# Two hybrid decoder layers: the rounded and the rest half of each weight chunk made by two DMAs and one ScalarE copy

## The chip, the cores and the metric

The kernel runs on one core of a Trainium2 chip. TensorE multiplies matrices, VectorE and ScalarE work on tiles element by element, GpSimd does small work of the same sort, and SyncE and GpSimd issue transfers (DMAs) between HBM and SBUF, the core's working memory. Each engine runs its own list of instructions in order and waits on semaphores for the others. The metric is the device time of one execution in microseconds; a time is the median of several runs.

## The reference

Two layers over 512 tokens of width 1024, all in float32. Cut to what matters here:

```python
for l in range(2):
    h = rms_norm(x, attn_norm_g[l])
    a_q, a_k, a_v, b_q, b_k, b_v, c_u, gates = split(h @ w_in[l])    # 1024 -> 9728 columns
    oa = diff_attention(rope(norm(a_q)), rope(norm(a_k)), a_v)       # 4 heads
    ob = dilated_window_attention(b_q, b_k, b_v)                     # 3 windows x 4 heads
    oc = s5_branch(c_u)                                              # state space scan, gated
    g = sigmoid(gates + b_gate[l])
    merged = g[0] * (oa @ w_br_a[l]) + g[1] * (ob @ w_br_b[l]) + g[2] * (oc @ w_br_c[l])
    x = x + merged @ w_out[l]
    a, b = split(rms_norm(x, ffn_norm_g[l]) @ w_up[l])               # 1024 -> 2 x 2816
    x = x + (silu(conv3(a)) * b) @ w_down[l]
```

The weights are 172 MB of float32, read once. The result has to keep float32 accuracy.

## The kernel before

TensorE multiplies in float32r, a float32 that is rounded to fewer bits. To keep the accuracy each operand is split into hi (the value rounded to float32r) and lo (what is left), and a product is the sum of three: hi\*hi, hi\*lo and lo\*hi (`mm3`, L172, products on L177 to L179). The activations are split when they are made (`hth` and `htl` for the normalised input, `gh` and `brh`/`brl` for others). The weights are split when they are loaded.

The weights come in 328 chunks of [128, 1024] float32 (512 KB), 164 in a layer, in the order in which the program wants them; the host packs them so. `chunk` (L151) makes the two halves: SyncE issues the load into a slot of the pool `raw` (3 slots, L155), ScalarE copies it to `whi` with rounding (5 slots, L158), and VectorE writes the difference raw - hi to `wlo` (5 slots, L159). A slot is free again when the last product that reads it has ended.

Chunks are used in two ways. In "t" and "t2" products (SSM input, gates and their branches, up projection) a chunk is used for 24 products in a row and is then done. In "n" products (`slab`, L162: q, k, v, output and down projection) three or four chunks make a slab of up to 1024 rows by 512 columns, and the slab is used for four tiles of 128 tokens, one after the other: each tile's pass goes through all chunks of the slab (6 products each), so a chunk is done only in the fourth pass. A boundary below is the place where one slab ends and the next begins.

Attention and the state space branch are side work: generators whose steps are put between the units of the projections (`tick`). The program is then given to a scheduling layer that sets each engine's order and all semaphores; GpSimd, ScalarE and VectorE each have one fixed list. GpSimd computes, among other things, the powers for the norms (`nr`, L410, of a tile of the input; `qr`, L477, of q and k heads) and clears buffers. At the start the input rows x are loaded by SyncE, ScalarE sums their squares (`junk`, L406), GpSimd makes the factor `nr`, VectorE the normalised rows `hn` (L413), TensorE transposes them (`ptp`, L184), and ScalarE and VectorE split them into `hth` and `htl`.

Of the kernel before, what the change touches and what calls it, by code (L numbers as in the profile page):

```python
"""Two hybrid decoder layers (differential attention, dilated window attention, S5 SSM, gated
merge, convolutional gated MLP) on one core.

float32 matrix products run as three float32r products: an operand is split exactly into
hi (rounded to float32r) and lo (the rest), and hi*hi + hi*lo + lo*hi accumulate in PSUM.
"""
# [10 lines left out]
F32 = mybir.dt.float32  # L17
# [3 lines left out]
AF = mybir.ActivationFunctionType  # L21
ALU = mybir.AluOpType
AX = mybir.AxisListType.X
MUL, ADD, SUB, MAX, MIN = ALU.mult, ALU.add, ALU.subtract, ALU.max, ALU.min
# [11 lines left out]
# S5 channels within a tile of 8 groups x 16 channels: partition = channel * 8 + group  # L36
UPERM = np.arange(512).reshape(4, 8, 16).transpose(0, 2, 1).reshape(512)

# columns of the small per-layer parameters
PK_BG, PK_GT, PK_SUB, PK_CW, PK_CB, PK_D, PK_BGLU, PK_N = 0, 24, 28, 29, 95, 117, 121, 125  # L40

BUFS = dict(raw=3, whi=5, wlo=5, qkv=20, acc=9, tmp=10, brh=1, brl=1, ct=1, gn=1)

# steps of side work per unit of a projection: SSM, attention
# [3 lines left out]
class Stream:  # L48
    """side work in steps: a step advances every running generator by one stage and starts the
    next one, so that the stages of successive generators are interleaved"""  # L50
# [26 lines left out]
class Alone:  # L77
    """a generator that starts when all before it have ended, and lets no other run beside it"""
# [5 lines left out]
class Net:  # L84
# [66 lines left out]
    def chunk(self, *spec):  # L151
        i = len(self.specs)
        self.specs.append(spec)
        raw = self.slot("raw", "raw", (128, 1024))
        self.nc.sync.dma_start(raw, self.io["wpk"][i])  # L155
        hi = self.slot("whi", "whi", (128, 1024), F32R)
        lo = self.slot("wlo", "wlo", (128, 1024), F32R)
        self.A.copy(hi, raw)  # L158
        self.V.tensor_tensor(lo, raw, hi.bitcast(F32), op=SUB)  # L159
        return hi, lo  # L160

    def slab(self, w, l, k0, nk, c0, before=None):  # L162
        """chunks for [nk*128, 512] of a weight; -> list over k of (hi, lo) [128, 512]"""
# [9 lines left out]
    def mm3(self, out, pairs):  # L173
        """out = sum over (stationary hi, lo), (moving hi, lo)"""
# [34 lines left out]
    def sincos(self, sin, cos, x, cols):  # L209
        """sin and cos of x [128, cols] (may overwrite x)"""  # L210
# [37 lines left out]
    def setup(self):  # L248
# [11 lines left out]
        # halves for sigmoids by tanh  # L260
# [3 lines left out]
        # columns for evacuating transposed q, k: gains times the score scale  # L264
# [5 lines left out]
        # angles: rope A (4 tiles x 8), rope B (2 orders x 4 tiles x 16), S5 (L x 16)  # L270
# [14 lines left out]
        # S5 scalars of both layers  # L285
# [18 lines left out]
        # f = (lambda - 1) / a  # L304
# [15 lines left out]
        # mag^8, and the unit phase exp(8 i theta)  # L320
# [12 lines left out]
    def layer_lambda(self, l):  # L333
        """lambda of the differential attention"""
# [17 lines left out]
    def layer_tables(self, l):  # L352
        """rope tables with gains and score scale; powers of the S5 lambda"""
# [17 lines left out]
        # powers of lambda, d = 0..8  # L371
# [8 lines left out]
    def cmul_step(self, tab, n, first, g):  # L380
        """tab[.., first+n : first+2n] = tab[.., first : first+n] * (element first+n-1 from `first`=1,
        or the n-th power kept apart): used for tables of powers that start at power 1"""
# [828 lines left out]
```

## Time and profile before

| | us |
|---|---|
| median of 3 runs (2149.47 to 2150.98) | 2149.77 |
| span of the profiled execution, first to last instruction | 2149.5 |
| TensorE busy | 2118.8 |
| VectorE busy | 1163.7 |
| ScalarE busy | 869.8 |
| GpSimd busy | 149.3 |

The profile gives the execution by its span; the median of the runs is 0.3 us above that. Busy times of engines overlap and don't add up to the span. A product's row lasts about 0.39 us while the next starts some 0.23 us later, since products are pipelined; distances between starts are what counts. The DMA share is the mean busy share of the core's 16 DMA engines. The TensorE clock was granted in full throughout (1.00).

### The profile page before, as it was taken

The page shows a single profiled execution, that of the slowest core. Times are in us where ns is not written, and L with a number is a line of the kernel's source. Part 1 is how long each engine was busy: PE and PEld are TensorE (multiplying, and loading weights), DVE is VectorE, ACT ScalarE, POOL GpSimd, SP SyncE. Part 2 cuts the span into 40 slices and gives each one's busy share as a digit, 9 for nine tenths or more (in the row PEclk, how much of TensorE's full clock was granted, in tenths as well). Part 3 has the DMA queues.
Part 4 walks back from the last instruction along what each step waited for, and adds up shares of the span by engine and source line. Part 5 has one row for each costly group of instructions (what it writes and reads, how often), then busy time and mean ns, then how long its engine had stood idle before and what let it go on. Part 6 is the DMA issues. An engine that isn't in the chain of part 4 may idle for free.

```text
span 2149.5 us, 28401 instructions
## 1 busy us (share of the span) xinstructions
PE 2118.8 (99%) x10742; PEld 1787.5 (83%) x10742; DVE 1163.7 (54%) x2589; ACT 869.8 (40%) x1789; POOL 149.3 (7%) x299
## 2 busy tenths in 40 slices
PE   7999999999999999999999999999999999999999
PEld 5877899988888888888888778999888888888887
DVE  6757565556544653544447575554564446445353
ACT  4355555463232432323334546464532324223131
POOL 1211111100000000000002102010000000000000
PEclk9999999999999999999999999999999999999999
DMA  5331221533433323323342312224334323233231
GB/s 185 99 100 40 60 81 59 136 113 99 137 98 93 108 92 95 98 89 98 118 123 64 96 42 68 85 68 123 113 108 129 102 73 108 88 106 92 77 118 59
DMA packets 97257, 206.40 MB, mean 96 GB/s; under 512 B 40544, under 2 KB 45408, under 8 KB 97120
## 3 DMA queue, kind: packets, MB, share of 16 engines
q1 hardware_dynamic: 97120, 204.58, 30.8%
q8 instruction: 85, 1.39, 0.3%
q14 instruction: 52, 0.43, 0.1%
HBM read 193.01 MB, written 11.53 MB: 95 GB/s over the span
## 4 chain that ended last, share of the span: by engine, by line
PE 88%; DVE 5%; ACT 4%; POOL 1%; DMA 1%; issue 1%; SPq 0%; ACTq 0%; DVEq 0%; POOLq 0%
PE pacc L179 26%; PE pacc L177 26%; PE pacc L178 26%; PE ptp L184 2%; PE ps L542 1%; PE po L639 1%; PE ps L615 1%; ACT qn L483 1%; PE ps L863 1%; DMA raw<-wpk 1%; ACT sq L474 1%; DVE wlo L159 1%; POOL qr L477 1%; PE ps L860 1%; PE ps L698 1%
## 5 line engine op out<-in xcount | busy, mean ns | idle before, releaser
L158 ACT CAST whi<-raw 128x1024 fp32r<-128x1024 f32 x328 | 343.7, 1054 | 676.6 <-PE pacc L178 403.9
L159 DVE TENSOR_TENSOR wlo<-raw,whi 128x1024 fp32r<-128x1024 f32 x328 | 399.0, 1223 | 401.0 <-ACT whi L158 394.4
L179 PE MATMUL pacc<-hth,wlo 128*128 128x512 f32 (+1 forms) x1200 | 460.7, 384 | 0.0
L177 PE MATMUL pacc<-hth,whi 128*128 128x512 f32 (+1 forms) x1200 | 458.6, 383 | 0.5 <-ACT hth L421 0.5
L178 PE MATMUL pacc<-htl,whi 128*128 128x512 f32 (+1 forms) x1200 | 458.7, 382 | 0.2
L177 PE MATMUL pacc<-whi,hth 128*128 128x512 f32 x768 | 319.8, 418 | 0.0
L178 PE MATMUL pacc<-wlo,hth 128*128 128x512 f32 x768 | 308.4, 402 | 3.2 <-DVE wlo L159 3.2
L179 PE MATMUL pacc<-whi,htl 128*128 128x512 f32 x768 | 310.4, 404 | 0.0
L178 PEld LDWEIGHTS pacc<-htl,whi 128*128 128x128 f32 x1200 | 225.4, 188 | 46.6 <-DVE htl L422 0.6
L177 PEld LDWEIGHTS pacc<-hth,whi 128*128 128x128 f32 x1200 | 225.1, 188 | 45.0 <-ACT hth L421 1.0
L179 PEld LDWEIGHTS pacc<-hth,wlo 128*128 128x128 f32 x1200 | 225.5, 188 | 43.8
L178 PEld LDWEIGHTS pacc<-wlo,hth 128*128 128x128 f32 x768 | 192.3, 251 | 18.9 <-DVE wlo L159 4.1
L179 PEld LDWEIGHTS pacc<-whi,htl 128*128 128x128 f32 x768 | 191.4, 249 | 16.5
L177 PEld LDWEIGHTS pacc<-whi,hth 128*128 128x128 f32 x768 | 191.3, 249 | 15.6 <-ACT hth L421 0.2
L177 PE MATMUL pacc<-whi,gh 128*128 128x512 f32 x352 | 139.9, 397 | 0.0
L178 PE MATMUL pacc<-wlo,gh 128*128 128x512 f32 x352 | 139.3, 396 | 0.0
L973 DVE TENSOR_TENSOR x<-x,pacc 128x512 f32<-128x512 f32 x64 | 44.0, 687 | 158.9 <-PE pacc L179 158.9
L178 PEld LDWEIGHTS pacc<-wlo,gh 128*128 128x128 f32 x352 | 66.1, 188 | 16.5
L177 PEld LDWEIGHTS pacc<-whi,gh 128*128 128x128 f32 x352 | 66.2, 188 | 16.0
L179 PE MATMUL pacc<-whi,brh 128*128 128x512 f32 x192 | 76.3, 397 | 0.0
L477 POOL TENSOR_TENSOR qr<-qr,mhalf 128x4 f32<-128x4 f32 (+1 forms) x64 | 75.6, 1181 | 5.3
L474 ACT ACTIVATE sq<-pacc 128x128 f32<-128x128 f32 x192 | 50.6, 284 | 41.1 <-PE pacc L179 40.9
(302 smaller groups left out, 2871.0 us busy)
## 6 DMA issues: line engine op xcount, KB each, us to landing
raw<-wpk SPq DMA_DIRECT2D x328, 512.0 KB, 3.7
x<-x SPq DMA_DIRECT2D x16, 256.0 KB, 6.0
gn<-ng SPq DMA_DIRECT2D x4, 512.0 KB, 5.8
u_d<-uS SPq DMA_DIRECT2D x8, 256.0 KB, 2.8
u<-u_d SPq DMA_DIRECT2D x8, 256.0 KB, 4.9
y_d<-ys SPq DMA_DIRECT2D x8, 256.0 KB, 2.2
ym<-y_d SPq DMA_DIRECT2D x8, 256.0 KB, 4.6
um<-u_d SPq DMA_DIRECT2D x8, 256.0 KB, 4.0
```

Source lines behind the costliest of these rows:

```text
L158: self.A.copy(hi, raw)
L159: self.V.tensor_tensor(lo, raw, hi.bitcast(F32), op=SUB)
L177: self.PE.matmul(out, lhsT=ah, rhs=bh, start=i == 0, stop=False)
L178: self.PE.matmul(out, lhsT=ah, rhs=bl, start=False, stop=False)
L179: self.PE.matmul(out, lhsT=al, rhs=bh, start=False, stop=i == n - 1)
L184: self.PE.transpose(tp[:, b * 128 : b * 128 + 128], src[:, b * 128 : b * 128 + 128], self.ident)
L474: A.activation(sq[:, h * dh : h * dh + dh], av[:, h], AF.Square, accum_out=ss[:, h : h + 1])
L477: G.tensor_tensor(r, r, self.mhalf[:, :heads], op=ALU.pow)
L483: A.activation(qv[:, h], qv[:, h], AF.Copy, scale=r[:, h : h + 1])
L542: PE.matmul(reg, lhsT=q[64 * j : 64 * j + 64, h * 128 : h * 128 + 128], rhs=k[kt][64 * j : 64 * j + 64, h * 128 : h * 128 + 128], start=kt ...
L615: PE.matmul(s[:, c : c + 128], lhsT=q[:, h * 128 : h * 128 + 128], rhs=k[kb][:, h * 128 : h * 128 + 128], start=h == h0 and b == 0, stop=F ...
L973: self.V.tensor_tensor(xt[t][s], xt[t][s], acc, op=ADD)
```

## The change

A chunk no longer has a raw slot. GpSimd issues a DMA that reads the float32 chunk and writes it to `whi` as float32r, so that the DMA does the rounding. ScalarE writes -hi into `wlo`. A second DMA, issued by GpSimd too, reads the same float32 chunk from HBM again and adds it onto that slot: `wlo` = raw - hi. VectorE's subtraction is gone. The three raw slots become two more for `whi` (7) and one more for `wlo` (6).

```diff
-BUFS = dict(raw=3, whi=5, wlo=5, qkv=20, acc=9, tmp=10, brh=1, brl=1, ct=1, gn=1)
+BUFS = dict(whi=7, wlo=6, qkv=20, acc=9, tmp=10, brh=1, brl=1, ct=1, gn=1)
...
     def chunk(self, *spec):
         i = len(self.specs)
         self.specs.append(spec)
-        raw = self.slot("raw", "raw", (128, 1024))
-        self.nc.sync.dma_start(raw, self.io["wpk"][i])
         hi = self.slot("whi", "whi", (128, 1024), F32R)
         lo = self.slot("wlo", "wlo", (128, 1024), F32R)
-        self.A.copy(hi, raw)
-        self.V.tensor_tensor(lo, raw, hi.bitcast(F32), op=SUB)
+        self.G.dma_start(hi, self.io["wpk"][i])
+        self.A.activation(lo, hi.bitcast(F32), AF.Copy, scale=-1.0)
+        self.G.dma_start(lo, self.io["wpk"][i], accum_op=ADD)
         return hi, lo
```

The rest of the diff takes out comments. Lines after the first few move by one: the load of hi is L156 of the changed kernel, the negated copy L157, the adding DMA L158.

What stands in the queues, at the two places that matter below. First the start. VectorE's list before begins with the subtraction of the first chunk, ahead of the cast of the identity and of the normalised rows hn:

```order
L159 TENSOR_TENSOR wlo_111<-raw_108,whi_110 128x1024
L243 CAST identr_69<-ident_64 128x128
L413 SCALAR_TENSOR_TENSOR hn_90<-x_73,nr_86,gn_77 128x512
L413 SCALAR_TENSOR_TENSOR hn_91<-x_75,nr_86,gn_77 128x512
L251 CAST identb_279<-identr_69 128x128
```

GpSimd's list in the changed kernel at the same place; `nr_86` is the factor of the first row tile (three instructions, L407 to L409), `whi_108`, `_144`, `_149`, `_154` and `wlo_109`, `_145` are the halves of the first four chunks:

```order
L156 DMA whi_108<-wpk 128x1024
masks.py:199 ISA
masks.py:199 AFFINE_SELECT ident_64<-ident_64 128x128
L407 TENSOR_TENSOR nr_86<-nss_81 128x1
L158 DMA wlo_109<-wpk 128x1024
L408 TENSOR_SCALAR nr_86<-nr_86 128x1
L156 DMA whi_144<-wpk 128x1024
L409 TENSOR_TENSOR nr_86<-nr_86,mhalf_71 128x1
L156 DMA whi_149<-wpk 128x1024
L156 DMA whi_154<-wpk 128x1024
L407 TENSOR_TENSOR nr_122<-nss_117 128x1
L158 DMA wlo_145<-wpk 128x1024
```

VectorE's hn no longer follows a subtraction, but the factor that it needs now ends behind the first adding DMA, which waits for the negated copy of the first chunk, and so do the loads of the chunks behind it.

Second, the boundary in the down projection of layer one. GpSimd's list in the changed kernel; `whi_8309`, `_8314`, `_8319` and `_8324` are the four chunks of the new slab, `wlo` with a number one higher their lo halves, `whi_8435` and `whi_8469` the next chunks:

```order
L156 DMA whi_8314<-wpk 128x1024
L158 DMA wlo_8310<-wpk 128x1024
L156 DMA whi_8319<-wpk 128x1024
L158 DMA wlo_8315<-wpk 128x1024
L156 DMA whi_8324<-wpk 128x1024
L158 DMA wlo_8320<-wpk 128x1024
L156 DMA whi_8435<-wpk 128x1024
L158 DMA wlo_8325<-wpk 128x1024
L156 DMA whi_8469<-wpk 128x1024
```

Before, SyncE's list held the loads into the raw slots at this place, one per chunk, and VectorE's the subtractions between the additions of the residual (`raw_8451` to `raw_8469` are the new slab's chunks):

```order
L973 TENSOR_TENSOR x_5952<-x_5952,pacc_8399 128x512
L159 TENSOR_TENSOR wlo_8460<-raw_8457,whi_8459 128x1024
L159 TENSOR_TENSOR wlo_8466<-raw_8463,whi_8465 128x1024
L159 TENSOR_TENSOR wlo_8472<-raw_8469,whi_8471 128x1024
L973 TENSOR_TENSOR x_5956<-x_5956,pacc_8425 128x512
```

The load of the fourth chunk (`whi_8324`) waits for the release of the first chunk of the old slab, seven chunks earlier; its adding DMA (`wlo_8325`) stands one load further on.

## Rows read from the trace of the kernel before

**Rows 1.** Page, part 1: busy time of each engine, share of the span, instructions.
```profile
PE 2118.8 (99%) x10742; PEld 1787.5 (83%) x10742; DVE 1163.7 (54%) x2589; ACT 869.8 (40%) x1789; POOL 149.3 (7%) x299
```

**Rows 2.** Page, part 5: line, operation | busy us, mean ns | idle before.
```profile
L158 ACT CAST whi<-raw 128x1024 fp32r<-128x1024 f32 x328 | 343.7, 1054 | 676.6 <-PE pacc L178 403.9
L159 DVE TENSOR_TENSOR wlo<-raw,whi 128x1024 fp32r<-128x1024 f32 x328 | 399.0, 1223 | 401.0 <-ACT whi L158 394.4
...
L477 POOL TENSOR_TENSOR qr<-qr,mhalf 128x4 f32<-128x4 f32 (+1 forms) x64 | 75.6, 1181 | 5.3
```

**Rows 3.** Waits of TensorE: who waited for whom, us in total, times, longest.
```profile
PE ptp L184 <- DVE hn L413: 13.2, 3, 12.5
PE pacc L178 <- DVE wlo L159: 3.2, 2, 1.6
```

**Rows 4.** DMA queue and weight loads: share; form, ns min/median/max; us to landing.
```profile
q1 hardware_dynamic: 97120, 204.58, 30.8%
...
L155 SPq DMA_DIRECT2D raw<-wpk x328: 327/328/3961, 2.1 to 2103.1; - x164
...
DMA to landing us min/median/max: 3.2/3.7/8.2
```

**Rows 5.** Timeline of ScalarE, up projection: start, us, engine, operation [idle before].
```profile
896.73 1.05 ACT L158 CAST whi<-raw 128x1024 fp32r<-128x1024 f32 x1 [3.90 <-PE pacc L178]
...
907.72 1.05 ACT L158 CAST whi<-raw 128x1024 fp32r<-128x1024 f32 x1 [3.90 <-PE pacc L178]
```

**Rows 6.** Timeline of TensorE, down projection: old slab’s first chunk, new slab’s fourth.
```profile
953.18 0.39 PE L179 MATMUL pacc<-whi,brh 128*128 128x512 f32 x1
...
962.05 0.39 PE L178 MATMUL pacc<-wlo,gh 128*128 128x512 f32 x1
```

**Rows 7.** Timeline of ScalarE at the same place.
```profile
953.62 1.05 ACT L158 CAST whi<-raw 128x1024 fp32r<-128x1024 f32 x1 [16.85 <-PE pacc L179]
955.02 1.05 ACT L158 CAST whi<-raw 128x1024 fp32r<-128x1024 f32 x1 [0.35 <-PE pacc L179]
956.42 1.06 ACT L158 CAST whi<-raw 128x1024 fp32r<-128x1024 f32 x1 [0.35 <-PE pacc L179]
959.79 1.06 ACT L158 CAST whi<-raw 128x1024 fp32r<-128x1024 f32 x1 [2.31 <-DMA raw<-wpk]
```

**Rows 8.** Timeline of TensorE: the same two products at the first and last boundary.
```profile
84.03 0.39 PE L179 MATMUL pacc<-whi,htl 128*128 128x512 f32 x1
...
93.32 0.40 PE L178 MATMUL pacc<-wlo,hth 128*128 128x512 f32 x1
...
2018.99 0.39 PE L179 MATMUL pacc<-whi,brh 128*128 128x512 f32 x1
...
2027.86 0.40 PE L178 MATMUL pacc<-wlo,gh 128*128 128x512 f32 x1
```

**Rows 9.** Timeline of the start.
```profile
6.00 0.56 POOL L410 TENSOR_TENSOR nr<-nr,mhalf 128x1 f32<-128x1 f32 x1
...
9.31 1.05 ACT L158 CAST whi<-raw 128x1024 fp32r<-128x1024 f32 x1 [4.42 <-DMA raw<-wpk]
...
10.39 1.23 DVE L159 TENSOR_TENSOR wlo<-raw,whi 128x1024 fp32r<-128x1024 f32 x1 [10.39 <-ACT whi L158]
...
11.67 1.41 DVE L413 SCALAR_TENSOR_TENSOR hn<-x,nr,gn 128x512 f32<-128x512 f32 x2
...
12.46 1.97 PE L184 MATMUL ptp<-identr,hn 128*128 128x128 f32 x8 [12.46 <-DVE hn L413]
...
17.70 0.39 PE L178 MATMUL pacc<-wlo,hth 128*128 128x512 f32 x1
```

**Rows 10.** Busy us (count) of PE, PEld, DVE, ACT, POOL; PEclk; DMA share; GB/s.
```profile
50.00:450.00 400.00, 394.24 (x2290) 348.48 (x2289) 250.84 (x765) 209.54 (x567) 62.61 (x111) 1.00 0.29 86
...
720.00:1075.00 355.00, 354.66 (x1582) 290.14 (x1581) 170.28 (x201) 112.48 (x143) 1.88 (x6) 1.00 0.32 100
...
1120.00:1515.00 395.00, 389.31 (x2267) 344.18 (x2266) 236.20 (x669) 207.16 (x565) 61.19 (x106) 1.00 0.28 83
```

## The prediction, made before the changed kernel ran

> **What bounds the kernel now.** I read the busy times first. TensorE is busy for 2118.8 of 2149.5 us, VectorE for 1163.7, ScalarE for 869.8, GpSimd for 149.3 [rows 1]. TensorE is the bound nearly everywhere, so work taken from VectorE saves time only where TensorE waits for it. Second, the table of waits: what TensorE itself waits for VectorE's lo half comes to 3.2 us in 2 waits, and 13.2 us go to the first transposes, which wait for the normalised rows hn [rows 3]. Third, the busy times by stretch: between 50 and 450 us TensorE is idle for 400 - 394.24 = 5.8 us, between 1120 and 1515 us, the same attention stage in layer two, for 5.7 us, and in the gated MLP between 720 and 1075 us for 0.3 us [rows 10]. All that can be won outside the start is therefore about 11.5 us, 0.5%.
>
> What can be lost is large: every product needs a chunk of weights, and a chunk lasts 2149.5 / 328 = 6.55 us on average. So the fourth reading was how long a weight slot takes from its release to its next need. In the up projection chunks are released every 5.5 us (three casts, each at a release, between 896.73 and 907.72) [rows 5], and with 6 slots a lo half has about five such steps, 27 us, to be made. The tight places are elsewhere. Where a slab of four chunks follows a slab of four with nothing between, all four slots of the old slab stay in use until its last token tile, and then come free 1.4 us apart.
>
> The clearest one is in the down projection. The last product that reads the first chunk of the old slab starts at 953.18; the first product that reads the lo half of the fourth chunk of the new slab starts at 962.05 [rows 6]. That is 8.87 us, for seven chunks further on: exactly the depth of the new hi pool. I matched all 8016 products with their chunks by the program's order and took this distance for every chunk. Twelve chunks (six in each layer, the same six) have 8.8 to 10.5 us: 9.3, 9.3, 10.5, 8.8, 9.0 and 8.9. The first of the twelve is 84.03 to 93.32, the last 2018.99 to 2027.86 [rows 8]. Two more have 11.8, six have 14 to 15, all others more than 17. TensorE's order in the changed kernel keeps these twelve boundaries.
>
> Before the change the same boundary was met because the raw chunk was already there: the cast starts at 953.62, 0.44 us after the last product's start, and the next ones at 955.02 and 956.42, one per release [rows 7]; cast and subtraction take 1.05 + 1.22 us [rows 2].
>
> **The change part by part.**
>
> VectorE loses 328 subtractions of 1223 ns, 399.0 us [rows 2]. On TensorE's path this is worth the 3.2 us of direct waits [rows 3]; I take -4, for some of the small waits in attention that follow from a shorter VectorE queue. The bounds are 0 and -11.5.
>
> ScalarE's cast of 1054 ns [rows 2] becomes a negated copy of the same 128x1024 elements, from SBUF to SBUF as before: same price, 0.
>
> SyncE loses 328 issues. GpSimd gains 656. An issue takes SyncE 0.33 us [rows 4]; GpSimd's nearest row is a 1.18 us instruction [rows 2]. I take 1.0 us: 656 us, and with its 149.3 us GpSimd stays below 40% busy. Nothing is lost by that alone. What matters is that its queue is in order: an accumulating DMA waits there for ScalarE's negated copy, and the next load and the small powers of the q and k norms stand behind it. By the order shown above the boundary loads stand in a workable sequence, so I add nothing for that except at the start.
>
> The chain of a chunk becomes serial: load, negated copy, second DMA. At the boundary: release (0.44 after the last product's start), load of hi, 0.05, copy 1.05, 0.05, second DMA. A plain chunk lands 3.7 us after its issue (3.2 to 8.2) [rows 4]; the trace has no load that rounds, none that adds, and none issued by GpSimd. For hi I take 3.7 + 1.0 for the issue = 4.7. The lower end is 3.7, the upper the slowest plain landing, 8.2. For lo the DMA must also read the slot that it adds to. A chunk occupies the 16 DMA engines for 30.8% x 2149.5 / 204.58 MB x 0.524 MB = 1.7 us [rows 4], so I take 4.7 + 1.7 = 6.4; lower end 3.7, upper 8.2 + 1.7 = 9.9.
>
> The chain is 0.44 + 4.7 + 0.05 + 1.05 + 0.05 + 6.4 = 12.7 us. Against the budgets TensorE is late by 3.4, 3.4, 2.2, 3.9, 3.7 and 3.8 in each layer, and 0.9 at the boundary of 11.8: 21.3, and twice that is **+43 us**. As a check by load: at 953.6 the engines get hi, lo, hi, lo, that is 1.7 + 3.4 + 1.7 + 3.4 = 10.2 us of work before the needed lo is there, which with the 2.0 us that a plain landing has beyond its 1.7 ends near 966, as the chain says (953.18 + 12.7 = 965.9). At the lower end the chain is 0.44 + 3.7 + 1.15 + 3.7 = 9.0 us, and the boundaries cost about 1 us in all; at the upper end it is 19.7 us, and the twelve and the eight next ones cost some 170.
>
> The Trainium skill, "DMA: Bandwidth & Descriptors", Latency and other measured facts, puts the first byte of a DMA issued by GpSimd at about 1 us and of one issued by SyncE at about 0.6. "Collectives: The Full Stack", in its passage on why ReduceScatter is half of AllGather, says that an adding DMA is slower through its second source read, not through the add. By these two, hi is 4.1 and lo 5.8, the chain 11.5, and the sum of the boundaries 26 instead of 43. No row of this trace shows either; the estimate is from those pages.
>
> The start. Before, GpSimd has the factor of the first row tile at 6.00 + 0.56; VectorE's first lo subtraction (10.39) stood ahead of hn (11.67), and the first transposes start at 12.46 [rows 9]. Now VectorE is free, but GpSimd's power stands behind the first lo DMA, which waits for the negated copy of the first chunk. That chunk landed at 9.31 [rows 9]; taken at about 8.2 now, the copy ends at 9.3, and the power follows behind two issues near 12.5. The transposes then start within a microsecond of where they did. The second chunk's load, too, stands behind that wait: issue 10.3, landing 15.0, copy 16.1, lo landing 22.5, where the first product with it started at 17.70 [rows 9]. I take +5 us, bounds 0 and +15.
>
> Sum: 2149.5 + 43 + 5 - 4 = **2193 us**. The span stands for the time: the median of the runs is 2149.8, 0.3 us above it.
>
> **The rivals.**
>
> *The halves land late by far more (B).* If an adding or a rounding DMA lands near the slowest row (8.2 and 9.9), the chain at a boundary is 16 to 19.7 us. At 16 the twelve lose 6.8 on average, the next two 4.2, the start some 10: 2149.5 + 82 + 8 + 10 = 2250; at 19.7 it is 2149.5 + 170 = 2320. For it: there will be about 5.1 us of DMA work per chunk of 5.5 us in the MLP, so transfers will queue. Against: 32% DMA share there now [rows 10].
>
> *The DMA engines become the bound (C).* In the MLP a chunk is wanted every 5.5 us [rows 5]. With 1.7 for hi, a lo that occupies the engines for more than 3.8 us (2.2 copies) can't keep up. At three copies it is 6.8 us a chunk: 328 x 6.8 = 2230, and the other transfers' 105 us (30.8% less the chunks' 84% of it) make 2335 us. Nothing in the trace excludes it; two copies is what must be moved.
>
> *It is hidden (D).* If both land in 3.7 us, the chain is 9.0 against budgets of 8.8 to 10.5: +1 there, +1 at the start, -4: 2147 to 2149.
>
> *It is faster (E).* As D, and the attention stages lose most of their 11.5 us of idle because VectorE's softmax and rope steps no longer queue behind subtractions: about 2139. It decides for itself only if landings stay below about 3.9 us, since one more microsecond in each costs twelve boundaries some 2 us each. Against it: hardly any TensorE wait in the table names VectorE's queue.
>
> **How the numbers follow.** Forecast 0.50 (its own range 2165 to 2225), B 0.15, C 0.15, D 0.12, E 0.08. A measurement of this kernel tells about 0.2%, 4.3 us, from no change. Faster is E: 0.08. Same is D: 0.12. Slower are the forecast, B and C: 0.80. The range leaves out E and most of C: 2146 to 2300.
>
> **What would show it.** VectorE's busy time falls to about 765 us, ScalarE's stays near 870. TensorE's waits name the lo half, with the DMA as releaser, at twelve boundaries (near 93, 238, 387, 692, 829, 962 us and again in layer two), 2 to 4 us each, and none in the up projection. The DMA share rises from 31% to about 80%. Wrong would be: waits for lo spread through the up projection (C), landings of lo beyond 8 us (B), or no wait for lo at all (D, E). If the waits stood on the powers of q and k, the in-order GpSimd queue would be the cause, which I have priced at nothing.

## The result, and the profile after

The changed kernel takes 2285.78 us (2278.14 to 2288.27), the kernel before 2150.18 beside it: ratio 1.0623 (95% interval 1.0605 to 1.0641), 136 us slower. The forecast was 44 us slower (2193). The direction was right, and the time lies inside the outer range of 2146 to 2300, but outside the forecast's own range of 2165 to 2225.

The page of the changed kernel, with its busy times, queues, two groups of instructions and landings:

```profile
PE 2161.0 (95%) x10742; PEld 1808.1 (79%) x10742; DVE 793.0 (35%) x2261; ACT 864.8 (38%) x1789; POOL 615.8 (27%) x955
...
q0 software_dynamic: 94464, 343.97, 67.2%
q1 hardware_dynamic: 49888, 32.59, 4.9%
...
L157 ACT ACTIVATE wlo<-whi 128x1024 fp32r<-128x1024 f32 x328 | 347.6, 1060 | 799.0 <-DMA whi<-wpk 544.4
L158 POOL DMA_DIRECT2D wlo<-wpk x328 | 287.4, 877 | 726.6 <-ACT wlo L157 685.6
...
whi<-wpk POOLq DMA_DIRECT2D x328, 512.0 KB, 6.6
wlo<-wpk POOLq DMA_DIRECT2D x328, 512.0 KB, 6.8
```

TensorE's idle time went from 30.7 us (2149.5 - 2118.8) to 124.1, and its busy time rose by 42.2 [rows 1]: it does the same 10742 products, so some ran slower. The mean granted clock of the span is 0.985 of the full one; 1.5% of 2285 is 34 us. ScalarE spends 544 us idle in front of copies whose hi load has not landed, GpSimd 686 us in front of adding DMAs whose copy is not done.

TensorE's waits (us, times, longest):

```profile
PE pacc L177 <- DMA wlo<-wpk: 62.7, 35, 4.3
PE ptp L183 <- DVE hn L412: 19.1, 4, 13.1
PE po L638 <- ACT pT L630: 10.4, 4, 4.4
PE ptp L560 <- DVE pa L556: 8.1, 6, 3.4
PE pacc L176 <- ACT hth L420: 8.0, 3, 5.9
PE ps L176 <- ACT zh L885: 8.0, 4, 3.8
```

The same view of the kernel before has, next to hn [rows 3]:

```profile
PE po L639 <- ACT pT L631: 1.8, 2, 0.9
...
PE ptp L561 <- DVE pa L557: 1.2, 2, 0.6
```

Two things are new: 62.7 us for lo, and waits for the normalised input and for side work (hn, pT, pa, hth, zh) that together are some 37 us longer than before.

The boundary of [rows 6] and [rows 7] now (timeline, several engines):

```profile
1023.33 0.39 PE L178 MATMUL pacc<-whi,brh 128*128 128x512 f32 x1
...
1024.03 0.55 POOL L156 DMA_DIRECT2D whi<-wpk  x1 [16.24 <-PE pacc L178]
1028.03 1.06 ACT L157 ACTIVATE wlo<-whi 128x1024 fp32r<-128x1024 f32 x1 [3.44 <-PE pacc L178]
1029.38 0.87 POOL L158 DMA_DIRECT2D wlo<-wpk  x1 [3.09 <-ACT wlo L157]
1032.53 0.50 PE L177 MATMUL pacc<-wlo,gh 128*128 128x512 f32 x1 [1.57 <-DMA wlo<-wpk]
...
1036.23 0.50 PE L177 MATMUL pacc<-wlo,gh 128*128 128x512 f32 x1 [2.04 <-DMA wlo<-wpk]
```

Release to first lo product: 12.9 us, where the prediction had 12.7. Hi takes 4.0, lo 6.85. TensorE is late twice, by 1.57 for the chunk ahead and by 2.04 for the fourth chunk, together 3.6 where the prediction had 3.9. This part went as described.

What had not been described stands 280 us earlier, at the slab change in the projection behind the merges (TensorE alone):

```profile
746.90 0.39 PE L176 MATMUL pacc<-whi,brl 128*128 128x512 f32 x1
751.61 0.50 PE L177 MATMUL pacc<-wlo,brl 128*128 128x512 f32 x1 [4.32 <-DMA wlo<-wpk]
...
752.45 0.63 PE L177 MATMUL pacc<-wlo,brl 128*128 128x512 f32 x1
752.88 0.63 PE L178 MATMUL pacc<-whi,ml 128*128 128x512 f32 x1
...
755.83 0.39 PE L176 MATMUL pacc<-whi,brh 128*128 128x512 f32 x1
```

After the wait, products start 0.43 us apart instead of 0.235, until 755.8: TensorE's clock is granted at the lower of its two levels, 1.2 GHz, in that stretch (mean granted clock from 752.4 to 755.8: 0.51), after 4.3 us of standing still. Products so spaced number 175 and lose 34.4 us together, the figure that the mean clock gives. The Trainium skill, "TensorE: Matmul & The Clock Gate", HAM oscillation, describes such a kernel, whose recurring waits for DMAs make it resume at half clock; by that rule about half of such a stretch is lost, and the trace agrees (0.195 of each 0.43 us).

And in the first attention stage, GpSimd's queue:

```profile
67.10 0.87 POOL L158 DMA_DIRECT2D wlo<-wpk  x1 [3.16 <-ACT wlo L157]
67.65 0.88 POOL L156 DMA_DIRECT2D whi<-wpk  x1
72.17 0.88 POOL L158 DMA_DIRECT2D wlo<-wpk  x1 [3.64 <-ACT wlo L157]
72.72 0.89 POOL L156 DMA_DIRECT2D whi<-wpk  x1
```

One chunk per 5 us. The hi load at 67.65 had its slot free at 60.7 but stood behind an adding DMA that waited for a copy that waited for the previous hi load. Issued right behind an adding DMA, it then takes 7.6 us to land. Over the trace, the 141 hi loads issued within 1 us of an adding DMA land in 7.6 us (median), the 121 issued more than 3 us after one in 4.2. Where the adding DMA is smaller, so is the delay: loads issued within 1 us of one land in 4.8 us behind 128 columns (e9 below) and in 6.3 behind 512 (e15). The Trainium skill, "DMA: Bandwidth & Descriptors", Queues, rings and completion order, describes a ring for each pair of queue row and DMA engine. If the two DMAs of GpSimd share a row, a load stands behind the adding DMA in the same rings; the medians agree with that, but no run here tests it alone.

Where the time is lost, by matching the first product of each chunk with that of before (us later than before; e2 to e13 are experiments below):

```
chunk, at (before)     after   no add  add 128  add 512  add elsewhere  fill MLP
   4     41.5           13.7     6.4      8.2      9.2        6.9         14.2
  56    465.5           55.0     5.1      9.8     34.0       41.7         53.3
 160   1048.7           74.3     5.2     16.1     44.8       48.7         65.0
 220   1531.3          118.7     5.6     17.5     62.2       87.4        108.3
 end   2149.5          135.5     5.8     21.3     73.4       96.5        120.3
```

Chunks 4 to 56 and 160 to 220 are mostly the attention stages, where the side work runs: 41 and 44 us. The rest, merges and MLP, loses 19 and 17: about 3 of each at the start of the up projection, whose first products wait for the normalised input, the others at boundaries. Within the up projection nothing is lost.

### The profile page after: what moved, and what is told of

It is laid out like the page before. It is cut to its first block, busy times and chain, and to the rows that moved or that the text cites. A ratio compares the mean times of both kernels' runs of the same rounds, so it can differ in the third digit from the quotient of the medians.

```text
span 2285.1 us, 28662 instructions
## 1 busy us (share of the span) xinstructions
PE 2161.0 (95%) x10742; PEld 1808.1 (79%) x10742; DVE 793.0 (35%) x2261; ACT 864.8 (38%) x1789; POOL 615.8 (27%) x955
## 3 DMA queue, kind: packets, MB, share of 16 engines
q0 software_dynamic: 94464, 343.97, 67.2%
## 4 chain that ended last, share of the span: by engine, by line
PE 54%; issue 19%; DMA 14%; POOL 6%; ACT 4%; DVE 3%; POOLq 0%; ACTq 0%; SPq 0%; DVEq 0%
PE pacc L177 16%; PE pacc L178 16%; PE pacc L176 16%; DMA whi<-wpk 7%; DMA wlo<-wpk 6%; POOL wlo L158 2%; POOL whi L156 2%; ACT wlo L157 1%; POOL qr L476 1%; PE ptp L183 1%; ACT sq L473 1%; PE ps L541 1%; DMA y_d<-ys 1%; PE ps L862 1%; ACT qn L482 0%
## 5 line engine op out<-in xcount | busy, mean ns | idle before, releaser
L157 ACT ACTIVATE wlo<-whi 128x1024 fp32r<-128x1024 f32 x328 | 347.6, 1060 | 799.0 <-DMA whi<-wpk 544.4
L158 POOL DMA_DIRECT2D wlo<-wpk x328 | 287.4, 877 | 726.6 <-ACT wlo L157 685.6
L156 POOL DMA_DIRECT2D whi<-wpk x328 | 224.3, 691 | 598.1 <-PE pacc L178 549.8
L177 PE MATMUL pacc<-wlo,hth 128*128 128x512 f32 x768 | 319.1, 416 | 40.2 <-DMA wlo<-wpk 40.1
L178 PE MATMUL pacc<-whi,htl 128*128 128x512 f32 x768 | 315.9, 411 | 0.0
L933 ACT ACTIVATE th<-pacc,hb 128x512 f32<-128x512 f32 x48 | 33.0, 688 | 129.8 <-PE pacc L178 123.9
```

Of the source, the lines that this page charges most:

```text
L156: self.G.dma_start(hi, self.io["wpk"][i])
L157: self.A.activation(lo, hi.bitcast(F32), AF.Copy, scale=-1.0)
L158: self.G.dma_start(lo, self.io["wpk"][i], accum_op=ADD)
L177: self.PE.matmul(out, lhsT=ah, rhs=bl, start=False, stop=False)
L178: self.PE.matmul(out, lhsT=al, rhs=bh, start=False, stop=i == n - 1)
L933: A.activation(th, gate, AF.Tanh, scale=0.5, bias=self.hb[:, l, 8 * b + f : 8 * b + f + 1])
```

## The experiments

All ratios are against the kernel before, run on the same chip.

| run | us | ratio, 95% interval | clock |
|---|---|---|---|
| after | 2285.8 | 1.0623 (1.0605 to 1.0641) | 0.985 |
| e1 fill | 2291.7 | 1.0653 (1.0638 to 1.0669) | 0.989 |
| e2 no add | 2155.9 | 1.0025 (1.0016 to 1.0035) | 0.998 |
| e3 copy on VectorE | 2293.4 | 1.0660 (1.0642 to 1.0678) | 0.980 |
| e4 traffic on before | 2209.7 | 1.0271 (1.0253 to 1.0288) | 0.990 |
| e5 unawaited, unpaced add | 2449.4 | 1.1381 (1.1364 to 1.1398) | 0.941 |
| e6 slabs old way | 2282.0 | 1.0609 (1.0586 to 1.0631) | 0.980 |
| e7 slabs new way | 2381.2 | 1.1057 (1.1028 to 1.1086) | 0.965 |
| e8 add alone | 2384.5 | 1.1068 (1.1049 to 1.1086) | 0.960 |
| e9 add 128 columns | 2170.0 | 1.0086 (1.0069 to 1.0103) | 0.998 |
| e10 loads first | 2320.7 | 1.0786 (1.0771 to 1.0801) | 0.979 |
| e11 round alone | 2200.9 | 1.0228 (1.0215 to 1.0242) | 0.994 |
| e12 fill MLP | 2275.1 | 1.0589 (1.0571 to 1.0608) | 0.987 |
| e13 add elsewhere | 2244.7 | 1.0429 (1.0405 to 1.0453) | 0.981 |
| e14 pools 5, 5 | 2589.7 | 1.2035 (1.2006 to 1.2065) | 0.942 |
| e15 add 512 columns | 2225.4 | 1.0350 (1.0323 to 1.0376) | 0.991 |
| e16 mixture, 2 / 6 / 5 | 2183.3 | 1.0148 (1.0132 to 1.0163) | 0.997 |
| e17 before, 2 / 6 / 5 | 2158.4 | 1.0035 (1.0023 to 1.0048) | 0.999 |
| e18 norms off GpSimd | 2277.6 | 1.0582 (1.0564 to 1.0600) | 0.979 |

### First four: which of three theories

Theory 1 says that products wait for lo at the boundaries, and that the clock falls behind such waits. Theory 2 says that the copy that waits for hi holds ScalarE's queue, and with it the side work. Theory 3 says that the load on the DMA engines makes every transfer late.

**e2, the adding DMA left out.**

```diff
-        self.G.dma_start(lo, self.io["wpk"][i], accum_op=ADD)
```

> The changed kernel without the adding DMA: lo stays the negated copy, so the second half of the split is left out. Theory 1: the chain at a slab change is 0.7 + 4.0 + 0.1 + 1.06 = 5.9 us, under the 8.8 to 10.5 that are there, so the 62.7 us of lo waits and most of the 34 us of low clock go; what is left above the kernel before is the start (8 to 10) and the side work: 2165 to 2180 us. Theory 2: the copy still waits for the hi load in ScalarE's queue, so the side waits (zh, pT, pa, hth, some 25 us more than before) stay: 2175 to 2180, the upper end. Theory 3: the DMA share falls by about 41 points to about 32%, transfers of the side work are as fast as before (y_d 2.2 us, um 4.0): 2150 to 2160.

2155.9 us: 130 of the 136 us go with the one line. What is left, the rounding load, ScalarE's copy that waits for it, 328 issues on GpSimd, costs 5.8 us, and all of it is there by chunk 4 (6.4): the start, as forecast (+5). ScalarE's wait for hi falls to a third, and hi lands in 4.0 (waits of ScalarE; the load's queue; landings of hi):

```profile
ACT wlo L157 <- DMA whi<-wpk: 186.1, 98, 3.9
...
q0 software_dynamic: 47232, 171.99, 27.3%
...
DMA to landing us min/median/max: 3.5/4.0/8.5
```

So theory 2 without the adding DMA falls; the adding DMA must be there.

**e3, the copy on another engine.**

```diff
-        self.A.activation(lo, hi.bitcast(F32), AF.Copy, scale=-1.0)
+        self.V.tensor_scalar(lo, hi.bitcast(F32), -1.0, None, op0=MUL)
```

> The changed kernel with the negated copy on VectorE instead of ScalarE; nothing is left out. Theory 2 (the copy that waits for the hi load holds ScalarE's queue, and with it zh, pT, pa and the hth casts at the start): these waits move off ScalarE, 15 to 25 us come back unless VectorE's own side steps now stand behind it: 2260 to 2270. Theory 1: the waits for lo and the clock stay as they are: 2280 to 2288. Theory 3: no change either.

Nothing comes back, 2293.4: the waits on pT, pa and zh nearly vanish, but lo costs 71.2 us and VectorE's own htl and zl some 14.

**e4, traffic that no product reads, on the kernel before.**

```diff
+        for _ in range(2):
+            d = self.dr.tile([128, 1024], F32, tag="scr", bufs=16, name=self.nm("scr"))
+            self.A.dma_start(d, self.io["wpk"][i])
```

> The kernel before, with two further DRAM-to-DRAM copies of each chunk, issued from ScalarE right after its cast: traffic that nothing waits for, which should take the DMA share from 31% to about 70%. Nothing of the computation is changed. Theory 3 (the load on the DMA engines is itself the cost): raw chunks land in 5 to 7 us instead of 3.7, the side transfers in 4 us and more, and the time rises by 20 us or more: 2170 to 2190. Theories 1 and 2: raw chunks are loaded three ahead, so the time stays within 2148 to 2158.

2209.7, more than expected of theory 3. Its two queues hold 71.7% of the engines, as the changed kernel does (72.1%):

```profile
q10 hardware_dynamic: 20992, 343.97, 44.3%
q1 hardware_dynamic: 97120, 204.58, 27.4%
...
raw<-wpk SPq DMA_DIRECT2D x328, 512.0 KB, 6.1
...
ym<-y_d SPq DMA_DIRECT2D x8, 256.0 KB, 9.3
um<-u_d SPq DMA_DIRECT2D x8, 256.0 KB, 7.7
```

By the same matching of chunks some 48 of 63 us are lost between chunks 4 and 56 and between 160 and 220, mostly attention, and 6 ahead of chunk 4. There transfers of the S5 state (um, ym) took 4.0 and 4.6 us before and take about twice that now. Two things keep the 59 us from being the price of load alone. ScalarE issues the copies, 656 times 0.50 us, in the same queue as its casts and side work; and the 16 scratch buffers are used again and again, so that by the profile ScalarE stands idle some 130 us in all until an earlier copy has landed. And the changed kernel's late transfers are others: its um and ym are no slower than before, u_d and y_d are (before, then after the change):

```profile
u_d<-uS SPq DMA_DIRECT2D x8, 256.0 KB, 2.8
...
y_d<-ys SPq DMA_DIRECT2D x8, 256.0 KB, 2.2
ym<-y_d SPq DMA_DIRECT2D x8, 256.0 KB, 4.6
um<-u_d SPq DMA_DIRECT2D x8, 256.0 KB, 4.0
```
```profile
u_d<-uS SPq DMA_DIRECT2D x8, 256.0 KB, 8.4
...
y_d<-ys SPq DMA_DIRECT2D x8, 256.0 KB, 4.0
ym<-y_d SPq DMA_DIRECT2D x8, 256.0 KB, 3.5
um<-u_d SPq DMA_DIRECT2D x8, 256.0 KB, 4.1
```

**e1, TensorE kept busy in the waits.** A table, `FILL`, says how many zero products stand ahead of the first lo product of which chunk; of the edit, the line that issues them:

```diff
+            for _ in range(self.fill.pop(id(bl), (0,))[0]):
+                self.PE.matmul(out, lhsT=ah, rhs=self.zero.broadcast_to([128, 512]), start=False, stop=False)
             self.PE.matmul(out, lhsT=ah, rhs=bl, start=False, stop=False)
```

> The changed kernel, with 259 more products on TensorE that add zero (a zero column repeated as the moving operand), 3 to 19 of them just ahead of the first lo product of each of 32 chunks, as many as fit into the wait seen there (64.5 us in all, 0.235 us each); nothing is left out. Theory 1 (the waits for lo at the slab changes, and a TensorE clock that is granted at 1.2 GHz for a stretch after such a wait): the 32 waits are filled, about 13 of the 17 low stretches inside the run vanish, each worth 1.7 us: 2285 - 22 = 2263 us (2255 to 2272), low stretches 68 us in all before, under 25 us now. Theory 2 (ScalarE's queue, held by the copy that waits for the hi load, delays side work) and theory 3 (the DMA engines' load delays every transfer) both say no change: 2282 to 2288, with the low stretches still there.

No gain. TensorE's idle for lo fell from 62.7 to 21.3 us, but 61 us of fill took its place: the counts were sized by the waits of one execution, and where a wait was shorter the fill itself was the delay. A bad size, no verdict on the clock; e12 is the same with less.

### Chain or load

From here on the theories are L, the load of the adding DMA on the engines; S, the serial chain, that is the products' own wait for lo; and Q, GpSimd's in-order queue.

**e9 and e15, an eighth and a half of the columns added.**

```diff
-        self.G.dma_start(lo, self.io["wpk"][i], accum_op=ADD)
+        self.G.dma_start(lo[:, :128], self.io["wpk"][i][:, :128], accum_op=ADD)
```

In e15 it is 512 for 128.

> The changed kernel, but the adding DMA adds only the first 128 of a chunk's 1024 columns; the rest of lo stays the negated copy, so seven eighths of the second half are left out. Every issue, wait and place in GpSimd's queue stays; of the adding DMA's load an eighth stays. Theory L (the load of the adding DMA on the engines is what costs): the DMA share falls to about 38% and the time to 2155 to 2190 us. Theory Q (GpSimd's queue is in order: the next chunk's hi load stands behind an adding DMA that waits for the copy, so a chunk takes about 5 us whatever the load): landings of lo 4 to 5 us, hi loads still held 5 to 8 us after their slot is free, waits for lo stay at slabs: 2215 to 2260 us.

> The changed kernel, but the adding DMA adds the first 512 of a chunk's 1024 columns; for the others lo stays the negated copy, so half of the second half is left out. With no adding DMA the time was 2156, with 128 columns 2170, with all 2286. Theory L: in proportion, 2156 + 130 / 2 = 2221 us (2210 to 2235). Theory S: lo lands in about 4.9 us instead of 6.8 (3.1 for 128 columns), the chain at a slab change is 11 us against 8.8 to 10.5, so 1 to 2 us late at twelve places, with few low stretches: 2180 to 2200 us.

2170.0 and 2225.4. All issues, waits and places in GpSimd's queue are there in e9, and of the 130 us 14 are left: the order of the queue alone (theory Q) is not the cost. From 0 over 128 and 512 to 1024 columns the loss beyond e2 is 0, 14, 69 and 130 us, about in proportion to the bytes (0, 16, 65, 130); the threshold that theory S has is not there. This is the loss as a whole: TensorE's waits for lo grow with the columns too (0, 11.4, 38.9, 62.7 us), so these runs don't divide it.

**e13, an adding DMA in the same place, but onto memory that nobody reads.** It reads the negated copy from SBUF and adds it onto DRAM; the first eight chunks fill the scratch buffers by a plain copy. (e5 was a first try at this, which added the raw chunk from HBM.) Of the edit:

```diff
-        self.G.dma_start(lo, self.io["wpk"][i], accum_op=ADD)
...
+            self.G.dma_start(self.scr[i % 8][:, :1024], lo.bitcast(F32), accum_op=ADD)
```

> The changed kernel, but the second DMA of a chunk adds the negated copy onto one of eight scratch buffers in DRAM that nothing reads, instead of adding the raw chunk onto lo; lo stays the negated copy, so the second half of the split is left out. Unlike the earlier run with unread adds, each stands at its place in GpSimd's queue, behind the copy of its chunk. The DMA share should stay near 70%. Theory L (load: hi loads and side transfers that come late): landings of hi stay near 6.6 us, 2200 to 2240 us, that is half or more of the 130 us that the adding DMA costs. Theory S (the products' own wait for lo): 2155 to 2185 us.

> The changed kernel with the adding DMA turned away: it adds the raw chunk onto one of eight scratch buffers in DRAM that nothing reads, and lo stays the negated copy, so the second half of the split is left out. The load on the DMA engines stays near 70%, but no product waits for an adding DMA. The copies of unread traffic cost 59 us on the kernel before, and leaving the adding DMA out gave back 130 of the 136 us. Theory L (its load is the larger part, by transfers of the side work that arrive late): 2200 to 2220 us, the loss all in the attention stages, none at the slab changes of the MLP. Theory S (the serial chain is the larger part, products wait for lo): 2155 to 2180 us.

e5 tells nothing of the changed kernel: its adds read only DRAM, so nothing paced them, they ran ahead and filled the engines in the first half of the span (landing 15.9 us). e13 is paced, and no instruction waits for its adding DMAs: 2244.7 us. Its landings, its queue and TensorE's waits:

```profile
whi<-wpk POOLq DMA_DIRECT2D x328, 512.0 KB, 6.5
scr<-wlo POOLq DMA_DIRECT2D x328, 512.0 KB, 6.8
...
q0 software_dynamic: 94464, 343.97, 70.0%
...
PE ptp L188 <- DVE hn L417: 24.2, 6, 13.8
PE ptp L565 <- DVE pa L561: 18.6, 6, 5.6
PE ps L181 <- ACT zh L890: 11.3, 4, 3.7
PE po L643 <- ACT pT L635: 8.0, 4, 3.2
```

No product waits for lo, and still 89 us more than e2. By the table above some 75 of the 89 fall between chunks 4 and 56 and between 160 and 220. The step from e13 to the changed kernel, in which products wait for lo, is the other 41 (2285.8 - 2244.7). The engines are 3 points busier than after the change, and the DMA adds in another direction, so 89 may be a little high. Part of it is clock: 1.9% of 2246 is 43 us, against 4 in e2.

**e11 and e8, either half alone,** both with the pools of the kernel before (raw=3, whi=5, wlo=5). e11, without the line of the pools:

```diff
+        raw = self.slot("raw", "raw", (128, 1024))
+        self.nc.sync.dma_start(raw, self.io["wpk"][i])
...
         self.G.dma_start(hi, self.io["wpk"][i])
-        self.A.activation(lo, hi.bitcast(F32), AF.Copy, scale=-1.0)
-        self.G.dma_start(lo, self.io["wpk"][i], accum_op=ADD)
+        self.V.tensor_tensor(lo, raw, hi.bitcast(F32), op=SUB)
```

e8 has the raw load too, and keeps copy and adding DMA:

```diff
-        self.G.dma_start(hi, self.io["wpk"][i])
+        self.A.copy(hi, raw)
```

> The other part of the change alone: hi comes by the rounding DMA from GpSimd, the raw chunk is still loaded by SyncE and VectorE subtracts as before; pools of 3, 5 and 5 as before. Nothing is left out. The chain from a slot's release is 0.7 + 4.0 + 0.1 + 1.2 = 6.0 us against 6.0 to 7.6 at a slab change for this depth, and no instruction of GpSimd waits for another engine's step in it. Theories Q and S: 2150 to 2165 us. Theory L: the DMA share is about 55%, between 33% (5 us lost) and 72% (59 to 136 us lost): 2165 to 2200.

> One part of the change alone: the raw chunk is loaded by SyncE three ahead and cast by ScalarE as before, and only lo is made anew, by a negated copy and the adding DMA; pools of 3, 5 and 5 as before. Nothing is left out. The chain from a slot's release is 0.44 + 1.05 + 1.06 + 0.1 + 6.8 = 9.5 us without a hi load in it, but the pool is two shallower, which takes about 2.8 us from the 8.8 to 10.5 of a slab change: about 3.5 us late each, as after the change; the DMA share is 3 points higher than after the change. Theories S and L: 2255 to 2300 us, so the rounding load is not what costs. If the rounding load were a main part: under 2220.

e11: 2200.9; theory L's upper end, with 53% of the engines in use and no add at all. TensorE waits for VectorE's lo in 14 waits, 11.0 us, so this is not load alone. e8: 2384.5, far over what was expected; TensorE waits for lo 53 times, 133.0 us. Its pools have two hi slots and one lo slot fewer than the changed kernel's, which would make the slow lo felt more; e8 alone does not show that this is the reason.

### Queue order, clock, depth

**e10 and e18, GpSimd's queue.** e10:

```diff
-        self.G.dma_start(hi, self.io["wpk"][i])
+        with self.tc.high_priority():
+            self.G.dma_start(hi, self.io["wpk"][i])
```

> The changed kernel with the hi loads issued at a higher priority: in GpSimd's queue three or four hi loads then stand ahead of the adding DMAs of a slab, where hi and lo alternated; in the up projection the order stays. Nothing is left out. Theory Q: the loads that were held 5 to 8 us in the attention stages go out when their slot is free; the 17 us of waits for lo outside the slab changes shrink, and the side work with them: 2235 to 2270 us. But an adding DMA can then stand behind a load that waits for a slot of the slab still in use, which would make lo late by up to a slab's last part: 2290 to 2340 us. Theory L: the traffic is the same, no change, 2280 to 2290.

e18, one of three like places:

```diff
-        G.tensor_scalar(r, ss, 1.0 / dh, EPS, op0=MUL, op1=ADD)
-        G.tensor_tensor(r, r, self.mhalf[:, :heads], op=ALU.pow)
+        self.V.tensor_scalar(r, ss, 1.0 / dh, EPS, op0=MUL, op1=ADD)
+        self.V.tensor_scalar(r, r, 0.0, 0.05, op0=MUL, op1=ADD)
```

> The changed kernel with the norms' small steps on VectorE instead of GpSimd; the inverse square root is left out, a constant stands in its place. GpSimd's queue then holds the 656 DMAs and memsets, no DMA waits behind a norm and no norm behind a DMA. Theory Q2 (the shared in-order queue of GpSimd carries the 89 us): 2286 - 50 to 2286 - 80, so 2205 to 2240 us. Theory H (the hi loads land late, at 6.5 us instead of 4.0, and hold ScalarE's queue): 2270 to 2288 us, with the hi landings still near 6.6 and TensorE's waits on hn, pa and pT as before.

e10: 2320.7, worse by 35: hi lands earlier (5.3) and lo later (7.5, with 83 us of waits). e18: 2277.6, 8 us better than the changed kernel: the norms in GpSimd's queue are a small part.

**e12, fill again, eleven chunks, 60% of each wait.** The edit is e1's with another table, which is:

```diff
+FILL = {97: 12, 120: 4, 121: 6, 144: 4, 145: 6, 260: 4, 261: 6, 284: 4, 285: 6, 308: 4, 309: 6}
```

> The changed kernel with zero products ahead of the first lo product, as in the first experiment, but only at eleven chunks of the merges and the gated MLP, whose waits were 1.7 to 4.5 us, and for about 60% of each wait, so that no product is added beyond the wait; nothing is left out. Theory 1 for the clock (a wait of this length lowers TensorE's granted clock to 1.2 GHz for 3.4 us, which costs 1.7 us): four of the five low stretches there go, 2286 - 7 = 2279 us (2275 to 2282). If the clock falls whatever TensorE does in the wait: 2284 to 2289, with the low stretches still behind these waits.

2275.1, 10.7 us better than the changed kernel; the single times, 2271.8 to 2284.9, overlap the changed kernel's 2278.1 to 2288.3, so the size of the gain is uncertain. Merges and MLP (chunks 56 to 160 and 220 to the end) lose 11.7 + 12.0 instead of 19.3 + 16.8, and the granted clock is full there (busy times by stretch, e12 and after; the column before the DMA share is the clock):

```profile
720.00:1130.00 410.00, 406.40 (x1845) 332.86 (x1845) 112.11 (x173) 124.17 (x164) 103.87 (x152) 1.00 0.81 183
```
```profile
720.00:1135.00 415.00, 401.61 (x1802) 328.46 (x1801) 112.63 (x175) 123.59 (x163) 103.20 (x152) 0.99 0.80 180
```

The waits for lo that are left (42.8 us) and the 62 zero products (14.6) come to 57.4 us against 62.7, and 1.3% of 2270 is 29.5 us of clock against 34: about half of the gain in the profiled executions is the clock, which holds where products that do nothing shorten the standstill, the rest shorter waits.

**e14, e6, e16, e17 and e7, the depth of the pools.**

```diff
-BUFS = dict(whi=7, wlo=6, qkv=20,
+BUFS = dict(whi=5, wlo=5, qkv=20,
```

That is e14. e17 is the kernel before with raw=2, whi=6, wlo=5. The mixtures, e6 (raw=3, whi=5, wlo=5) and e16 (2, 6, 5):

```diff
+        if spec[0] == "n":
+            raw = self.slot("raw", "raw", (128, 1024))
+            self.nc.sync.dma_start(raw, self.io["wpk"][i])
+            self.A.copy(hi, raw)
+            self.V.tensor_tensor(lo, raw, hi.bitcast(F32), op=SUB)
+            return hi, lo
         self.G.dma_start(hi, self.io["wpk"][i])
```

e7 has `!=` there (1, 6, 6).

> The changed kernel with pools of 5 hi and 5 lo slots instead of 7 and 6; nothing is left out. The load per chunk is the same. Theory S: a slab change has 2.8 us less, 12 x 2.8 = 34 us and as many low stretches of the clock, and the changes that had 14 to 16 us to spare come in as well; slots in the up projection last 5 x 5.5 = 27 us against a chain of 15, so nothing there: 2330 to 2400 us. Theory L: the load is spread over a slightly longer time, 2285 to 2300 us.

> A mixture: the 156 chunks of slabs (half of the 328) are loaded by SyncE, cast by ScalarE and subtracted by VectorE as before the change, with pools of 3, 5 and 5; the other 172 chunks, of the up projection and the gates, are made by the two DMAs as after it. Nothing is left out. Theory S (the lo waits at slabs, and what follows from them): nothing left to wait, 2150 to 2158 us. Theory L: the attention stages hold mostly slab chunks, so their transfers are as fast as before; the MLP carries no side work with transfers: 2150 to 2165. If instead every adding DMA costs alike, half of the loss stays: about 2215.

> The mixture turned round: the 156 slab chunks by the two DMAs as after the change, the other 172 by load, cast and subtraction as before it, with pools of 1 raw, 6 hi and 6 lo slots. Nothing is left out. The hi pool is one shallower than after the change, so a slab change has 1.4 us less: 12 x 1.4 = 17 us against it. Theories S and L both put the loss at slabs: 2265 to 2305 us. If every adding DMA costs alike: about 2225.

> The mixture with slabs made the old way and the other 172 chunks by the two DMAs, with pools of 2 raw, 6 hi and 5 lo slots instead of 3, 5 and 5; nothing is left out. With 5 and 5 slots it stood 10.9 us behind the kernel before at 409 us and lost 56 us more in the merges and the gated MLP of layer one. Depth theory: one more hi slot gives 5.5 us more there, against a chain of 13 to 15 us and 5 slots of 5.5: most of that loss goes, 2165 to 2215 us. If the adding DMAs cost whatever the depth: 2260 to 2290.

> The kernel before with pools of 2 raw, 6 hi and 5 lo slots instead of 3, 5 and 5; nothing is left out and no DMA changed. The chain there is a cast and a subtraction, 2.3 us, against 6.0 to 7.6 us at the slab changes, so a slot more or less should be worth nothing: 2147 to 2152 us. If depth as such pays here, the 3.2 us of waits for lo go and it is 2145 or less.

e14 takes 2589.7, 304 us more than with 7 and 6 slots, far beyond what either theory gave:

```profile
PE pacc L177 <- DMA wlo<-wpk: 198.9, 77, 6.4
PE pacc L178 <- DMA wlo<-wpk: 32.8, 20, 3.6
```

The second line has lo as the moving operand: mostly the gates and the up projection, which with 7 and 6 slots never waited. e6 was missed, it seems, for the same reason: it is only 10.9 us behind the kernel before at chunk 48, in the attention stage, but at 5 and 5 slots the merges and the MLP lose. One more hi slot in place of a raw slot (e16) brings it from 2282.0 to 2183.3, with 8 us of lo waits. On the kernel before a slot moved from raw to hi costs 7 us (e17). e7, at 2381.2, is over its expectation too: 45 waits for lo, 123.6 us, on a hi pool of six. None of the versions beats the kernel before.

## Why the prediction was wrong, step by step

- **Slab changes, +43: right.** At the boundary shown the chain was 12.9 for 12.7, its lo 6.8 for 6.4, its hi 4.0 for 4.7. The waits at the twelve announced boundaries, with the chunk just ahead of each, are 20 and come to 41 us in the trace. That the step from e13 to the changed kernel is 41 too is a coincidence: it holds all 62.7 us of waits for lo, against other waits and low clock that e13 has more of.
- **The estimate from two pages of the Trainium skill ("DMA: Bandwidth & Descriptors", Latency and other measured facts; "Collectives: The Full Stack", why ReduceScatter is half of AllGather): half right.** At the boundary hi landed as the estimate says (4.1 against 4.0), lo did not (5.8 against 6.8), and here the measurement decides; over the whole trace hi takes 6.6, which neither the estimate nor the forecast's 4.7 has. By the queue's shares in the traces, if the rounding load costs what it does in e2, the adding DMA holds the engines 2.89 us ((67.2% x 2285.1 - 27.3% x 2155.4) / 328) and the rounding load 1.79: 1.6 times, where I priced 3.4 and 1.7.
- **Start, +5: right without the add (e2), 13.7 with it,** by the fourth chunk. The transposes start at 13.13 us, as described. But the second chunk's copy waits for its hi until 19.46, where the prediction had 15.0, and the first hth casts stand behind it in ScalarE's queue; TensorE waits 5.9 us for them.
- **VectorE, -4: not seen.** e2 has the same VectorE relief, and behind its start it gains at most some 2 us on the kernel before, which are lost again.
- **"I add nothing for that except at the start": the step that failed.** The prediction priced GpSimd's queue, and the DMA engines' load below saturation, at nothing away from the boundaries. An adding DMA costs 89 us there with no product waiting for its result (e13 less e2), most of them in the attention stages. What the trace shows of the way: hi loads behind adding DMAs land in 7.6 us instead of 4.2; ScalarE, whose queue also carries pT, zh and the hth casts, is idle for them 544 us instead of 186; side work comes late by a few microseconds at a time. That the loss follows the adding DMA's bytes, and not its issue, its wait or its place in the queue, is shown (e9, e15). Taking one thing out of one queue gives little back (the copy out of ScalarE's, e3, nothing; the norms out of GpSimd's, e18, 8 us), which does not exclude the queues together. How the 89 divides between late hi loads and late side transfers stays open; of the state's transfers above only u_d is much later in e13 than before (8.5 us instead of 2.8).
- **The clock: not in the prediction at all.** 34 us of the 136 are products at 1.2 GHz after waits. They are no further term: e2 has 4 of them, e13 43, so some 39 of the 89 us are clock, and the step of 41 has 9 less of it. [rows 10] showed 1.00 throughout, and I carried that over to a kernel that I expected to wait.
- **The announced signs.** The up projection does not wait: right, so rival C falls. Lo waits at the boundaries: right, but there are 35 waits for lo, 1.8 us on average; the 15 that are not at the announced places (22 us) are at the start and in the attention stages. DMA share 72%, not 80. TensorE's waits do not stand on the powers of q and k, and e18 gives back 8 us only, so GpSimd's norms are not the cause. The time lies between rival B's 2250 and 2320, but not by B's mechanism: at the boundary the chain took 12.9 us, not 16 to 19.7. Landings of lo beyond 8 us, B's sign, are there, 23 of 328.

## What to carry to other kernels

A chain made longer is not priced at its tight places alone. If it goes through an in-order queue that other work shares, or puts its bytes in front of the next load, look also at that other work: here the stretches that are mostly attention lost 85 us, and the up projection, whose lo halves have 27 us to be made in, nothing. Before trusting a sum over the tight places, price a change's bytes by a run that moves them with nobody waiting (e13; e4 shows how hard that is to get clean). And a wait that TensorE newly gets can cost more than its length, where it resumes at the lower clock.

## What was not expected of the hardware

The wait of 4.3 us at 751.6 is followed by products 0.43 us apart, those of 1.6 and 2.0 us at 1032.5 and 1036.2 are not. The length of the wait does not decide it alone: after two waits of 1.5 and 2.0 us, at 894.1 and 897.8, products are 0.43 us apart too. With zero products in the waits of the merges and the MLP the granted clock stays full there (e12). The kernel's loss grew about in proportion to the adding DMA's columns, from 128 to 1024. And pools two and one slots shallower (5 and 5 for 7 and 6) cost 304 us, more than twice the change itself.
